# Gate panel 0 instead of gate panel 5 among the early products, in a fused hybrid-encoder step on one Trainium2 core

## The chip, the core and the metric

One core of one Trainium2 chip runs the whole program. The metric is the device time of one execution in microseconds (us). TensorE (PE) does matrix products, VectorE (DVE) and ScalarE (ACT) element-wise work, GpSimd (POOL) small work and some transfers, SyncE (SP) issues most DMAs. Each engine takes its instructions strictly in the order in which they were written for it.

## The reference

One layer, for 1024 prompt positions and 64 sample positions (together T = 1088), D = 1024 channels:

```
xn = rms_norm(x, g_pre);  z = xn @ w_in
xa, ga, q, k, v, gb, fl, ma, mb = split(z)
ua = causal_conv(xa)                          # width 4, per channel
r, i = sigmoid(block_diag(ua) + bias)         # two gates
a = exp(-8 r softplus(-a_param));  x_in = sqrt(1 - a^2) * i * ua
h_t = a_t h_(t-1) + x_in_t                    # the recurrence
ya = h * silu(ga)                             # branch a
yb = attention(q, k, v, logf) * silu(gb)      # branch b
mix = (sigmoid(ma) * (ya @ w_a) + sigmoid(mb) * (yb @ w_b)) @ w_o
h = x + rms_norm(mix);  h += rms_norm(sigmoid(h @ w_ple_gate) * (p @ w_ple_proj))
```

Branch a has 1024 channels, treated as eight panels of 128 channels, numbered 0 to 7. For panel k there is an x panel (columns of xa, the input of convolution and recurrence) and a gate panel (columns of ga, which multiply the recurrence's output through silu). Each is a product of the 1088 normalised positions with 1024 x 128 weights.

## The kernel before

All products are made in a split of float32 into a high and a low part, as three matmuls (high x high, low x high, high x low; lines L166 to L168). The stages that matter follow each other on TensorE.

**Products of halves.** Query and key columns go in pairs of panels through a Strassen-like scheme with seven products of half size (`seven`, L811, tiles `quad`). Four panels of branch a are made there too, two at a time: the x panel 0 with gate panel 1 in front of the queries and keys, and gate panels 3 and 5 behind them. Their results go to memory: x panel 0 to `d_x0`, gate panel k, with silu already applied, to `d_ga[k]`. Which gate panels are made early is in one table, `GA_EARLY`.

**Attention**, with dense panels of the merge gates as filler. It ends where the first panel of the next stage begins.

**The recurrence of branch a.** What is not made early is made here as *dense panels*: a panel is 72 matmuls, three chunks of columns (368, 368 and 352 wide) of 24 each, tile `acc`, and each chunk takes one of the 8 PSUM banks (`mm8`) until another engine has read it out. The list of dense panels is written out in the order x1, g0, x2, x3, g2, x4, x5, g4, x6, x7, g6, g7 (x for an x panel, g for a gate panel). For each of the eight k the steps are:

- the x panel's chunks are copied from PSUM to the tile `xp` (ScalarE, L84);
- convolution: one ScalarE step (`u<-xp`, L1662) and three on VectorE (L1666); for odd k the tiles carry an `_e`, for even k they don't;
- `u` is split into `uh` (ScalarE) and `ul` (VectorE);
- six small products for the two gates (tiles `gacc`, three matmuls each, one bank each), read out by six sigmoids on ScalarE (L1705, into `x` and `r`);
- decay and root: exponential (L1720), tanh (L1723), square root (L1740) on ScalarE; sigmoid, exponential/tanh and square root need different function tables, and a change of table is an `ACT_TABLE_LOAD`;
- state input and scan on VectorE (L1750, L1746, L1762), output y = h * silu(gate) (L1781), split into `yah` (ScalarE) and `yal` (VectorE);
- the gate panel: where it is dense, a sigmoid on ScalarE (L1811, `sg<-acc`) and a product on VectorE (L1814), which only then frees the bank; where it was made early, one DMA on SyncE's queue loads it from `d_ga` (L1821). The tile `sg` exists twice, for even and for odd k.

The order in which these steps are written for the engines is not fixed by hand: `go_all` is a list scheduler. It holds for each step an engine, a duration, what it depends on, the need for a free bank and the function table, and always takes the step that can begin first by these numbers, ties going to the step with the longest chain behind it. Dense panels stay in their order. Steps issued by TensorE take half a chunk (12 matmuls) or one gate product at a time.

**Held products.** The outputs `yah`, `yal` are multiplied with the first two panels of branch a's output projection (tiles `held`); the further panels, branch b's projection, the output projection and the final embedding stage follow on TensorE.

The lines that the change reaches:

```
GA_EARLY = (1, 3, 5)                                                     # L50
some = [(cols(C_XA, 1), ("r", d_x0))] + [(cols(C_GA + k * P, 1), ("g", d_ga[k])) for k in GA_EARLY]   # L227
mixed = [([s1, s2], (d1, d2)) for (s1, d1), (s2, d2) in (some[:2], some[2:])]
for k in range(KT):                                                      # the list of dense panels
    branch_a += [("x", k + 1)] if k + 1 < KT else []
    branch_a += [("g", k)] if k not in GA_EARLY else []
...
        if k in GA_EARLY:                                                # L1823, own_gate(k)
            step("S", 500.0, load, w=sgs(k), lag=4000.0)
        else:
            dense(("g", k), evac)
```

Of the kernel before, what the change touches and what calls it, by code (L numbers as in the profile page):

```python
# [46 lines left out]

AHEAD = 4000
WAKE = 30
GA_EARLY = (1, 3, 5)  # L50
LN1P = [1.0 / 15, 1.0 / 13, 1.0 / 11, 1.0 / 9, 1.0 / 7, 1.0 / 5, 1.0 / 3]


# [14 lines left out]
def hybrid_step(tc, a, o):  # L68
# [151 lines left out]
    def cols(c, n=2):  # L220
        return w_in[:, c:c + n * P]
# [4 lines left out]
    quads = [([cols(c + p * P)], ((t, p), (t, p + 1))) for p in range(0, NP, 2) for c, t in ((C_K, "k"), (C_Q, "q"))]  # L226
    some = [(cols(C_XA, 1), ("r", d_x0))] + [(cols(C_GA + k * P, 1), ("g", d_ga[k])) for k in GA_EARLY]  # L227
    mixed = [([s1, s2], (d1, d2)) for (s1, d1), (s2, d2) in (some[:2], some[2:])]
# [6 lines left out]
    for k in range(KT):  # L235
        branch_a += [("x", k + 1)] if k + 1 < KT else []
        branch_a += [("g", k)] if k not in GA_EARLY else []
    later = deque([(cols((C_XA if t == "x" else C_GA) + k * P, 1), ((t, k),)) for t, k in branch_a]
# [1224 lines left out]
    def step(engine, ns, do, r=(), w=(), lag=0.0, after=(), table=None, bank=0, ahead_of=0.0, frees=False):  # L1463
        i = len(todo)
        deps = set(after)
        for x in (*r, *w):
            deps |= {written[x]} if x in written else set()
        for x in w:
            deps |= read_by.get(x, set())
        for x in w:  # L1470
            written[x], read_by[x] = i, set()
        for x in r:
            if x not in w:
                read_by.setdefault(x, set()).add(i)
        todo.append((engine, ns, do, deps, lag, table, bank, ahead_of, frees))
        return i
# [61 lines left out]
    def sgs(k):  # L1538
        return [("sg", odd(k), c) for c in range(3)]
# [261 lines left out]
    def own_gate(k):  # L1801
# [20 lines left out]

        if k in GA_EARLY:  # L1823
            step("S", 500.0, load, w=sgs(k), lag=4000.0)
# [704 lines left out]
```

## Time and profile before

| what | us |
|---|---|
| three runs | 1425.78, 1425.80, 1425.51; median 1425.78 |
| the profiled execution: its span | 1425.7 |
| TensorE busy in it | 1401.0 (98%) |
| the recurrence and the held products, from the first dense panel to the last held product | 844.4 to 1034.0 |

The profiled execution's span, from its first to its last instruction, is within 0.1 us of the median of the runs, so nothing of weight lies around it. Times in rows are from the start of the span. Matmuls overlap: a row's duration is from its issue to its end, while the distance between the starts of neighbours tells the pace (368 columns: 0.17 us). An entry `[1.35 <-DVE y L1254]` at the end of a row is idle time of the engine before it and what ended it.

### The profile page before, as it was taken

The numbers are of one execution on the slowest core, as the hardware profiler recorded it, in microseconds if no ns is written. First come the engines' busy times: TensorE is split into PE (matmuls) and PEld (weight loads), VectorE is DVE, ScalarE is ACT, GpSimd is POOL, SyncE is SP. The second block draws the span as 40 slices with busy tenths as digits, with TensorE's granted clock in tenths as the row PEclk, the third lists the DMA queues.
The fourth block names the chain that finished last, engine by engine and source line by source line (L and its number), as shares of the span: only waits on it lengthen the run. The fifth ranks groups of instructions, "written<-read, shape, count | busy, mean of one in ns | idle before, by whom it ended". The sixth has DMA issues, their size and how long they took to land.

```text
span 1425.7 us, 24345 instructions
## 1 busy us (share of the span) xinstructions
PE 1401.0 (98%) x9063; PEld 1331.9 (93%) x9063; DVE 901.7 (63%) x1563; ACT 728.6 (51%) x1338; POOL 379.7 (27%) x485
## 2 busy tenths in 40 slices
PE   9999999999999999999999899999999999999996
PEld 8999999999999999999999889999999998888885
DVE  6546665665653466667676567798845866338644
ACT  5414444444332566666666558778624434324533
POOL 0002332423321355455544430010001564000000
PEclk9999999999999999999999999999999999999999
DMA  5376655655336858757567434242283667224111
GB/s 204 123 131 109 114 168 178 189 158 171 95 76 183 217 150 148 177 125 178 131 155 163 65 89 57 44 61 48 79 299 126 213 215 281 91 76 146 49 49 44
DMA packets 141074, 191.64 MB, mean 134 GB/s; under 512 B 24580, under 2 KB 99372, under 8 KB 140956
## 3 DMA queue, kind: packets, MB, share of 16 engines
q1 hardware_dynamic: 119308, 149.43, 42.7%
q10 hardware_dynamic: 17104, 27.32, 5.3%
q0 software_dynamic: 4544, 13.34, 3.3%
q8 instruction: 71, 1.16, 0.4%
q14 instruction: 47, 0.39, 0.1%
HBM read 127.11 MB, written 62.92 MB: 133 GB/s over the span
## 4 chain that ended last, share of the span: by engine, by line
PE 89%; DMA 5%; DVE 2%; ACT 1%; issue 1%; SPq 1%; POOL 0%; DVEq 0%; ACTq 0%; POOLq 0%
PE quad L811 19%; PE acc L166 13%; PE acc L167 12%; PE acc L168 12%; PE quad_b L2129 5%; PE tp L1196 4%; PE pv L1240 2%; PE pv L1238 2%; PE s L1171 2%; PE s L1170 2%; DMA d_ma<-st 1%; PE vacc L166 1%; DMA w_raw<-in_w_in 1%; PE vacc L167 1%; PE vacc L168 1%; DMA d_y<-y 1%
## 5 line engine op out<-in xcount | busy, mean ns | idle before, releaser
L166 PE MATMUL acc<-xh,wh 128*128 128x368 f32 (+1 forms) x672 | 228.0, 339 | 0.4
L167 PE MATMUL acc<-xl,wh 128*128 128x368 f32 (+1 forms) x672 | 220.1, 328 | 0.0
L168 PE MATMUL acc<-xh,wl 128*128 128x368 f32 (+1 forms) x672 | 219.7, 327 | 0.0
L166 PEld LDWEIGHTS acc<-xh,wh 128*128 128x128 f32 x672 | 126.8, 189 | 1.9 <-DVE nm L1150 1.3
L167 PEld LDWEIGHTS acc<-xl,wh 128*128 128x128 f32 x672 | 127.0, 189 | 0.6
L168 PEld LDWEIGHTS acc<-xh,wl 128*128 128x128 f32 x672 | 126.7, 189 | 0.0
L84 ACT ACTIVATE th<-tp 128x512 fp32r<-128x512 f32 (+1 forms) x160 | 86.6, 549 | 65.9 <-PE tp L1196 61.5
L87 DVE TENSOR_TENSOR tl<-tp,th 128x512 fp32r<-128x512 f32 (+1 forms) x160 | 99.2, 634 | 30.4 <-ACT th L84 29.1
L87 DVE TENSOR_TENSOR wl<-w_raw,wh 128x1024 fp32r<-128x1024 f32 (+1 forms) x67 | 76.8, 1148 | 59.6 <-ACT wh L84 40.8
L84 ACT ACTIVATE wh<-w_raw 128x1024 fp32r<-128x1024 f32 (+1 forms) x67 | 62.7, 938 | 91.2 <-PE quad L811 37.5
L811 PE MATMUL quad<-xh,wh 128*128 128x272 f32 x448 | 93.9, 291 | 0.0
L811 PE MATMUL quad<-xl,wh 128*128 128x272 f32 x448 | 92.6, 288 | 0.0
L811 PE MATMUL quad<-xh,wl 128*128 128x272 f32 x448 | 92.5, 288 | 0.0
L1156 POOL TENSOR_SCALAR pb<-pb,sm 128x640 f32<-128x640 f32 (+1 forms) x64 | 61.4, 960 | 95.1 <-DVE sm L1155 87.3
L1238 PE MATMUL pv<-tl,vv 128*128 128x512 f32 x192 | 70.8, 369 | 6.1 <-DVE y L1254 5.4
L1153 ACT ACTIVATE pb<-pb,nm 128x640 f32<-128x640 f32 (+1 forms) x64 | 63.3, 989 | 25.9 <-DVE nm L1150 23.2
L84 ACT ACTIVATE wh<-s 128x512 fp32r<-128x512 f32 x54 | 34.0, 631 | 74.6 <-PE quad L811 48.3
L811 PEld LDWEIGHTS quad<-xl,wh 128*128 128x128 f32 x448 | 70.6, 188 | 0.0
L811 PEld LDWEIGHTS quad<-xh,wh 128*128 128x128 f32 x448 | 70.2, 188 | 0.2
L811 PEld LDWEIGHTS quad<-xh,wl 128*128 128x128 f32 x448 | 70.4, 188 | 0.0
L1150 DVE CUSTOM_DVE_ANT_0 pb<-s,mask 128x640 f32<-128x640 f32 (+1 forms) x64 | 65.0, 1015 | 4.4 <-PE s L1171 4.2
L1170 PE MATMUL s<-k,q 128*128 128x128 f32 (+2 forms) x192 | 67.4, 358 | 0.0
(692 smaller groups left out, 3958.5 us busy)
## 6 DMA issues: line engine op xcount, KB each, us to landing
w_raw<-in_w_in SPq DMA_DIRECT2D x56, 256.0 KB
q<-d_q SPq DMA_DIRECT2D x48, 256.0 KB
k<-d_k SPq DMA_DIRECT2D x48, 256.0 KB
w_raw<-in_w_in SPq DMA_DIRECT2D x56, 128.0 KB
wraw<-in_w_in SPq DMA_DIRECT2D x24, 256.0 KB
w_raw<-in_w_branch SPq DMA_DIRECT2D x24, 256.0 KB
d_k<-oh ACTq DMA_DIRECT2D x16, 272.0 KB
d_k<-kl SPq DMA_DIRECT2D x16, 272.0 KB
```

Of the source, the lines that this page charges most:

```text
L84: return act.activation(out=out, in_=in_, func=AF.Copy, scale=scale)
L87: return eng.tensor_tensor(out=out, in0=in0, in1=in1, op=ALU.subtract)
L166: pe.matmul(out, ah, bh, start=start, stop=False)
L167: pe.matmul(out, ah, bl, start=False, stop=False)
L168: pe.matmul(out, al, bh, start=False, stop=stop)
L811: pe.matmul(acc[:, c, :CW], l[:, k, :], r[:, k, c * CW:(c + 1) * CW], start=(first and k == 0 and p == 0), stop=(k == 3 and p == 2), skip_ ...
L1150: at = book("D", now[0] + HOP_PE, per(D_MAX, n), lambda: dve.tensor_tensor_reduce(out=pr[:, :n], in0=s[:, :n], in1=m, scale=-1.0, scalar=- ...
L1153: at = book("A", at, per(A_EXP, n), lambda: act.activation(out=pr[:, :n], in_=pr[:, :n], func=AF.Exp, scale=-1.0, bias=nm, accum_out=sm))
L1156: return free, book("G", at, per(G_NORM, n), lambda: pool.tensor_scalar(out=pr[:, :n], in0=pr[:, :n], scalar1=sm, scalar2=1.0, op0=ALU.mul ...
L1170: pe.matmul(s[:, c0:c0 + w], t["q1"][:, q], t["k1"][:, c0:c0 + w], start=True, stop=False)
L1238: pe.matmul(pv[:, 512 - n:], v, tl[:, c:c + n], start=(j == 0), stop=False)
L2129: pe.matmul(acc[:, c, :CW], l[:, k, :], r[k // 2][:, k % 2, c * CW:(c + 1) * CW], start=(first and k == 0 and p == 0), stop=(k == 3 and p ...
```

## The change

The table of early gate panels names panel 0 in place of panel 5, in the same position:

```
-GA_EARLY = (1, 3, 5)
+GA_EARLY = (1, 3, 0)
```

So among the products of halves gate panel 0 is made together with gate panel 3, from other columns of the same weight matrix into `d_ga[0]`; and in the recurrence the list of dense panels reads x1, x2, x3, g2, x4, x5, g4, x6, g5, x7, g6, g7, while panel 0's gate is loaded and panel 5's no longer is. The numbers of matmuls, of DMAs and of steps stay the same. Up to the first dense panel every engine's instructions stand in the same order as before. Behind it the scheduler comes to another order on every engine. Three places of it follow; in them `u`, `r`, `x` without and with `_e` are the tiles for even and odd k.

SyncE's queue at the start of the recurrence (`sg` and `sg_e` are the tiles for the gate, `w_raw` a dense panel's weights, `g_raw` the small gate weights), as a piece of the difference:

```order
 L1821 DMA sg_e<-d_ga 128x1088
 L249 DMA w_raw<-in_w_in 128x2x128 x4
+L1821 DMA sg<-d_ga 128x1088
 L1613 DMA g_raw<-in_w_rg_a 64x64 x2
 L1613 DMA g_raw<-in_w_rg_x 64x64 x2
```

The load of gate panel 0 stands behind the first weights that this stage loads; the load of panel 5, further down, is gone.

ScalarE around the six sigmoids of k = 3 (`r_e<-gacc`, `x_e<-gacc`), before:

```order
L1720 ACT_TABLE_LOAD
L1720 ACTIVATE e<-r,nsp_93 128x1092
L84 ACTIVATE wh<-w_raw 128x1024
L1723 ACTIVATE r<-r,sp_92 128x1092
L1705 ACT_TABLE_LOAD
L1705 ACTIVATE r_e<-gacc,vt 128x368 x2
L1705 ACTIVATE x_e<-gacc,vt 128x368
L1705 ACTIVATE r_e<-gacc,vt 128x356
L84 ACTIVATE xp<-acc 128x368
L1705 ACTIVATE x_e<-gacc,vt 128x368
L1705 ACTIVATE x_e<-gacc,vt 128x356
L1811 ACTIVATE sg<-acc 128x368
```

The same place in the change, in two pieces that follow each other, the first from the copy of the second chunk of x4:

```order
L84 ACTIVATE xp<-acc 128x368
L1720 ACT_TABLE_LOAD
L1720 ACTIVATE e<-r,nsp_93 128x1092
L1723 ACTIVATE r<-r,sp_92 128x1092
L84 ACTIVATE wh<-w_raw 128x1024
```

```order
L84 ACTIVATE xp<-acc 128x288
L84 ACTIVATE xp<-acc 128x64
L1662 ACTIVATE u<-xp,vt 128x1092
L84 ACTIVATE fin<-xp 128x3 x2
L1705 ACT_TABLE_LOAD
L1705 ACTIVATE r_e<-gacc,vt 128x368 x2
L1705 ACTIVATE x_e<-gacc,vt 128x368
L1705 ACTIVATE r_e<-gacc,vt 128x356
L1705 ACTIVATE x_e<-gacc,vt 128x368
L1705 ACTIVATE x_e<-gacc,vt 128x356
L84 ACTIVATE uh<-u 128x1092
L1811 ACTIVATE sg<-acc 128x368
```

Two copies of x4 and the first step of the next convolution now stand between the tanh and the six sigmoids; the sigmoids of gate panel 2 (`sg<-acc`) stand behind the six in both.

TensorE at the same place in the change, from the fourth of the six gate products on (what a row waits for is in brackets; Activation is ScalarE):

```order
L166 MATMUL gacc<-uh,g_h 128x356 [waits Activation_49]
L167 MATMUL gacc<-ul,g_h 128x356
L168 MATMUL gacc<-uh,g_l 128x356
L166 MATMUL gacc<-uh,g_h 128x368 [waits PE_49,Activation_49]
L167 MATMUL gacc<-ul,g_h 128x368
L168 MATMUL gacc<-uh,g_l 128x368
L166 MATMUL gacc<-uh,g_h 128x356 [waits Activation_49]
L167 MATMUL gacc<-ul,g_h 128x356
L168 MATMUL gacc<-uh,g_l 128x356
```

The six products stand in one run directly behind the third chunk of x4; before, the first four stood behind a half chunk of x4, and 12 dense matmuls stood between the fourth and the fifth.

ScalarE at the six sigmoids of k = 5, before:

```order
L1740 ACT_TABLE_LOAD
L1740 ACTIVATE r<-r 128x1092
L84 ACTIVATE xp<-acc 128x368 x2
L1705 ACT_TABLE_LOAD
L1705 ACTIVATE r_e<-gacc,vt 128x368
L1705 ACTIVATE x_e<-gacc,vt 128x368
L1705 ACTIVATE r_e<-gacc,vt 128x368
L1705 ACTIVATE x_e<-gacc,vt 128x368
L1811 ACTIVATE sg<-acc 128x368
```

and in the change, where the first row copies the second chunk of x6:

```order
L84 ACTIVATE xp<-acc 128x368
L1740 ACT_TABLE_LOAD
L1740 ACTIVATE r<-r 128x1092
L1705 ACT_TABLE_LOAD
L1705 ACTIVATE r_e<-gacc,vt 128x368
L1705 ACTIVATE x_e<-gacc,vt 128x368
L1705 ACTIVATE r_e<-gacc,vt 128x368
L1705 ACTIVATE x_e<-gacc,vt 128x368
L1705 ACTIVATE r_e<-gacc,vt 128x356
L1705 ACTIVATE x_e<-gacc,vt 128x356
L1811 ACTIVATE sg<-acc 128x368 x2
```

The square root and its table now stand behind that copy, and all six sigmoids stand together. On TensorE the six products of k = 5 stand in one run behind the second chunk of x6 in the change. In all, ScalarE has 50 table loads where it had 47.

## The prediction

> **What bounds the kernel now.** The page first: who is busy, and for how long.
>
> ```profile
> span 1425.7 us, 24345 instructions
> PE 1401.0 (98%) x9063; PEld 1331.9 (93%) x9063; DVE 901.7 (63%) x1563; ACT 728.6 (51%) x1338; POOL 379.7 (27%) x485
> ```
>
> TensorE sets the time; what an edit gains or costs is what it takes from or adds to TensorE's waits. The change moves instructions only behind the first dense panel of the recurrence, so next the stretch table for that stage, and the waits of TensorE behind it (engine, line, what it waited for; us in total, times, longest):
>
> ```profile
> 844.40:1034.00 189.60, 189.60 (x1151) 189.60 (x1150) 155.96 (x162) 143.12 (x220) 15.93 (x39) 1.00 0.34 64
> PE acc L166 <- DVE s L2148: 1.0, 1, 1.0
> PE quad_b L2129 <- DVE s L2148: 0.3, 1, 0.3
> ```
>
> In the stage (columns: length, then busy us of PE, PEld, DVE, ACT, POOL, granted clock, DMA share, GB/s) TensorE is busy for all 189.60 us. There is no wait to remove, and the change takes no matmul away. From 1034 to the end TensorE waits 1.3 us. Two things follow. The change can gain at most about 1.3 us, and a wait that it puts into this stage goes to the end almost whole, because nothing behind it has slack to swallow it. The question is whether the new order makes TensorE wait.
>
> **The change part by part.**
>
> *What costs nothing.* The early product of panel 0 has the shape of panel 5's, in the same place: 0. The dense panel g5 has the 72 matmuls of g0: 0, as long as TensorE does not wait. VectorE and ScalarE do the same steps; the three more table loads at 1.28 us (rows below) are 3.8 us, and ScalarE idles for 189.6 - 143.1 = 46.5 us in the stage. That cover holds except where TensorE waits for a ScalarE step queued behind a table load; those places are priced below. On SyncE's queue the 544 KB load of `sg` now stands behind the first four weight loads; queued behind it are the small gate weights and the next panel's weights. Those came late for ScalarE before, too:
>
> ```profile
> 856.62 1.06 ACT L84 ACTIVATE wh<-w_raw 128x1024 fp32r<-128x1024 f32 x1 [2.21 <-DMA w_raw<-in_w_in]
> 857.71 1.22 DVE L87 TENSOR_TENSOR wl<-w_raw,wh 128x1024 fp32r<-128x1024 f32 x1 [2.69 <-ACT wh L84]
> ```
>
> They are split by 858.9, for the third panel, which TensorE begins two panels (2 x 11.8 us, 72 matmuls each) and 12 gate products (some 6 us) after 844.4, at 874. Some 15 us of slack, and the DMA share of the stage is 0.34: 0.
>
> *The first wait: gate products of k = 3.* There are 8 banks. In the change the six products stand directly behind the third chunk of x4. At that moment gate panel 2 holds three banks, since its own sigmoids stand behind the six on ScalarE; the first five products take the other five. The sixth can begin only when the first of the six sigmoids has read its bank out. When does TensorE arrive, and when is the sigmoid done? As TensorE never waits before this place, in either program, the same count of matmuls brings it to the same time, and I read the times off the rows of before. Up to the first product it has 414 matmuls behind it (five dense panels and three groups of 18): the 415th is the row at 912.61. The last matmul of the second chunk of x4 is the one at 908.58.
>
> ```profile
> 844.43 0.33 PE L166 MATMUL acc<-xh,wh 128*128 128x368 f32 x1
> ...
> 908.58 0.33 PE L168 MATMUL acc<-xh,wl 128*128 128x368 f32 x1
> ...
> 912.61 0.33 PE L166 MATMUL acc<-xh,wh 128*128 128x368 f32 x1
> ...
> 914.60 0.33 PE L166 MATMUL gacc<-uh,g_h 128*128 128x368 f32 x1
> ...
> 916.61 0.33 PE L166 MATMUL acc<-xh,wh 128*128 128x368 f32 x1
> ```
>
> From 914.60 to 916.61 four products take 2.01 us, so five take 2.51 and TensorE stands before the sixth at 912.61 + 2.51 = 915.12. On ScalarE everything between is queued behind the copy of x4's second chunk, which cannot start before that chunk ends, at 908.58 + 0.33 = 908.91. Then, from start to start in rows where the same steps follow each other:
>
> ```profile
> 865.51 1.28 ACT L1720 ACT_TABLE_LOAD   x1
> 866.81 1.21 ACT L1720 ACTIVATE e<-r,nsp 128x1092 f32<-128x1092 f32 x1
> 868.05 1.21 ACT L1723 ACTIVATE r<-r,sp 128x1092 f32<-128x1092 f32 x1
> 869.28 1.28 ACT L1705 ACT_TABLE_LOAD   x1
> ...
> 897.81 1.06 ACT L84 ACTIVATE wh<-w_raw 128x1024 fp32r<-128x1024 f32 x1 [2.97 <-PE acc L167]
> 898.77 0.51 ACT L84 ACTIVATE xp<-acc 128x288 f32<-128x288 f32 x2
> 899.37 1.31 ACT L1662 ACTIVATE u_e<-xp,vt 128x1092 f32<-128x1092 f32 x1
> 900.58 0.28 ACT L84 ACTIVATE fin<-xp 128x3 f32<-128x3 f32 x2
> 900.80 0.42 ACT L84 ACTIVATE g_h<-g_raw 128x256 fp32r<-128x256 f32 x1
> ...
> 924.18 0.46 ACT L84 ACTIVATE xp<-acc 128x368 f32<-128x368 f32 x1
> 924.53 1.20 ACT L1723 ACTIVATE r_e<-r_e,sp 128x1092 f32<-128x1092 f32 x1
> ...
> 942.42 1.28 ACT L1705 ACT_TABLE_LOAD   x1
> 943.71 0.57 ACT L1705 ACTIVATE r<-gacc,vt 128x368 f32<-128x368 f32 x1
> ```
>
> Copy 0.35 (924.18 to 924.53); table, exponential and tanh 3.77 (865.51 to 869.28); weight split, two copies, convolution step and two small copies 2.99 (897.81 to 900.80); table and first sigmoid 1.86 (942.42 to 943.71 + 0.57). Sum 8.97, so the bank is free at 917.88: **2.76 us** of wait. Before, the same sigmoids started 1.5 us after their first product (914.60), and the last two products came later by 12 matmuls:
>
> ```profile
> 914.83 1.28 ACT L1705 ACT_TABLE_LOAD   x1
> 916.12 1.02 ACT L1705 ACTIVATE r_e<-gacc,vt 128x368 f32<-128x368 f32 x2
> ```
>
> *The second wait: gate products of k = 5.* The same picture: gate panel 4 holds three banks, five products the others, and the sixth needs the first sigmoid. The six stand behind the second chunk of x6, 642 matmuls after the start: the row at 950.28, the one ahead of it at 950.12, both now 2.76 later.
>
> ```profile
> 950.12 0.33 PE L168 MATMUL acc<-xh,wl 128*128 128x368 f32 x1
> 950.28 0.32 PE L166 MATMUL acc<-xh,wh 128*128 128x352 f32 x1
> ...
> 983.92 1.28 ACT L1740 ACT_TABLE_LOAD   x1
> 985.22 1.12 ACT L1740 ACTIVATE r_e<-r_e 128x1092 f32<-128x1092 f32 x1
> 986.24 0.40 ACT L84 ACTIVATE g_h<-g_raw 128x256 fp32r<-128x256 f32 x1
> ```
>
> TensorE stands before the sixth at 950.28 + 2.76 + 2.51 = 955.55. ScalarE's chain begins with the copy of x6's second chunk, at 950.12 + 0.33 + 2.76 = 953.21: copy 0.35, table and root 2.32 (983.92 to 986.24), table and first sigmoid 1.86, sum 4.53, done at 957.74: **2.19 us**. Before, root and table lay ahead of the copies, and no product waited.
>
> *Starting again.* After an idle stretch the first two matmuls are further apart than usual: 0.34 us where 0.23 is the pace of 512 columns.
>
> ```profile
> 839.12 0.50 PE L1238 MATMUL pv<-tl,vv 128*128 128x512 f32 x1 [1.35 <-DVE y L1254]
> 839.46 0.40 PE L1240 MATMUL pv<-th,vv 128*128 128x512 f32 x1
> 839.69 0.60 PE L1196 MATMUL tp<-ident,pb 128*128 128x128 f32 x4
> ```
>
> That is 0.1 us for each wait, together 0.2.
>
> *What is late next.* The dense panels behind the waits, the held products and everything behind 1034 move by the sum. ScalarE and VectorE work on x2 to x5 one panel (11.8 us) earlier than before, which would help only where TensorE waits for them; in this stage it did so nowhere.
>
> *Sum.* 2.76 + 2.19 + 0.2 = 5.15 on the profiled execution's 1425.7 is 1430.9; its span is within 0.1 us of the median of the runs, 1425.78, so against that too **1430.9 us**, 0.36% more.
>
> *Bounds of what the trace does not show.* No wait for a bank by a gate product of this size stands in the trace of before. From below each of the two is 0, if a bank comes free otherwise; a gain is excluded, since TensorE has nothing left to save there. From above: a ScalarE step in the chain may itself be held by VectorE, and the longest such wait in the stage is
>
> ```profile
> ACT uh L84 <- DVE u L1666: 11.6, 3, 4.1
> ```
>
> 4.1 us, which at one of the places gives 1430.9 + 4.1 = 1435.0. I take the chains as summed: all their rows are plain back-to-back steps, and both start from an end of TensorE's own work.
>
> **The rivals.**
>
> *The banks come free in time, no wait: 1425.8, not slower.* The place is the sixth product of k = 3. It decides itself by ScalarE's chain: TensorE needs 915.12 - 908.91 = 6.2 us from the end of x4's second chunk to the sixth product, and the wait is gone when the chain takes no more than that instead of 8.97. For it: before, TensorE passed all eight gates without a wait. Against it: engines work in order, the chain's first step is a copy of a chunk that TensorE has only just made, and leaving out even the whole convolution step (1.31) and the weight split (1.06) leaves 6.6. At k = 5 the same would need 4.53 to come down to 2.3. One wait without the other gives 1428.0 (only the second) or 1428.6 (only the first).
>
> *The wait costs TensorE its clock.* In the trace of before one idle stretch is followed by half the granted clock (the column ahead of the DMA share), a shorter one (1.35 us, above) is not:
>
> ```profile
> 809.00 0.79 PE L1238 MATMUL pv<-tl,vv 128*128 128x512 f32 x1 [4.05 <-DVE y L1254]
> 808.00:812.00 4.00, 3.00 (x11) 2.70 (x12) 3.72 (x14) 3.03 (x10) 0.77 (x2) 0.50 0.00 0
> 812.00:816.00 4.00, 4.00 (x19) 3.92 (x18) 1.75 (x4) 2.31 (x5) 1.28 (x2) 0.69 0.01 2
> ```
>
> 4.05 us of idleness cost half of 3.0 busy us and 0.31 of 4.0: 2.7 us. The first wait, 2.76, lies between 1.35 and 4.05; if it were enough, the time would be 1430.9 + 2.7 = 1433.6. Being nearer the lower of the two, and the second wait shorter still, I give it little. [...]
>
> *The chain is longer (VectorE holds ScalarE):* 1435.0, as bounded above.
>
> *Faster.* The earlier x panels would have to take away waits of TensorE; behind 844 there are 1.3 us, so 1424.5 at best, which is no change that can be told.
>
> **How the numbers follow.** About 0.2% (2.9 us) is what a measurement of this kernel can tell from no change. Forecast, both waits: 0.72. No wait: 0.08; one wait: 0.08 (about on the border, two thirds of it within 0.2%). Clock: 0.04. Longer chain: 0.05. Faster in some way that I don't see: 0.03. Slower is then 0.72 + 0.04 + 0.05 + 0.03 = 0.84, less a little for waits of which each comes out half a microsecond or more shorter: 0.82. Within 0.2%: 0.15, faster 0.03. The likeliest case's own range is 1429.3 to 1432.5 (each wait give or take some 0.7, the two sums of durations being good to about that). The range for 8 in 10 reaches down to the single waits and up to the clock case: 1428.0 to 1434.0.
>
> **What would show it.** TensorE's waits in the stage: two at L166 on `gacc`, each ended by ScalarE's sigmoid L1705, 2.8 us near 918 and 2.2 us near 958; the first held product at 1015.6 instead of 1010.5; nothing new behind it; granted clock 1.00 in the stage. Wrong if no `gacc` wait stands there, if a wait has another releaser (weights `wl`, a DMA, `ul`), or if the held products begin 5 us late and the end does not.

## The result, and the profile after

The changed kernel took 1428.88 us (median of 21 runs, 1424.38 to 1431.93) beside 1425.58 us (1423.59 to 1427.41, 21 runs) of the kernel before: a ratio of 1.0022, 95% interval 1.0016 to 1.0029. That is 3.3 us slower, inside the predicted range and 2.0 us below the predicted time. The two waits that were forecast came, but the sum around them was wrong in two places that nearly cancel, so the closeness of the number is in part luck. One execution of experiment 5 took 1719.66 us at a granted clock of 0.751 and is left out of the comparisons.

First the page of the changed kernel's profiled execution (1428.84 us, span 1427.1), then TensorE's waits in the recurrence, and those behind it:

```profile
span 1427.1 us, 24346 instructions
PE 1401.5 (98%) x9063; PEld 1333.2 (93%) x9063; DVE 903.1 (63%) x1563; ACT 733.6 (51%) x1341; POOL 378.2 (26%) x485
...
PE gacc L166 <- ACT r_e L1705: 5.1, 2, 2.7
...
PE acc L166 <- DVE s L2148: 1.0, 1, 1.0
PE quad_b L166 <- DVE s L2000: 0.7, 1, 0.7
```

The recurrence has two new waits, and both are where the prediction put them: at the sixth gate product of k = 3 and of k = 5, ended by the first of ScalarE's sigmoids. Their rows in the timeline, with the last matmul ahead of each:

```profile
907.28 0.33 PE L168 MATMUL gacc<-uh,g_l 128*128 128x368 f32 x1
910.31 0.43 PE L166 MATMUL gacc<-uh,g_h 128*128 128x356 f32 x1 [2.70 <-ACT r_e L1705]
...
949.55 0.32 PE L168 MATMUL gacc<-uh,g_l 128*128 128x356 f32 x1
952.24 0.66 PE L166 MATMUL gacc<-uh,g_h 128*128 128x356 f32 x1 [2.37 <-ACT r_e L1705]
```

Now the recurrence whole, from its first matmul to the first held product, before and after (columns as in the stretch table above):

```profile
844.43:1010.51 166.08, 166.08 (x1010) 166.08 (x1009) 135.38 (x140) 131.25 (x203) 12.15 (x32) 1.00 0.33 56
836.67:1011.50 174.83, 169.76 (x1010) 169.06 (x1009) 142.22 (x147) 137.59 (x209) 12.36 (x34) 0.98 0.33 58
```

It became 8.75 us longer, not 5.15. It also began 7.76 us earlier, and what stands behind it takes 415.63 instead of 415.20 us. So -7.76 + 8.75 + 0.43 makes the +1.4 us by which the two profiled executions differ. (The runs differ by 3.3 because the first profile of before is of a dear execution: a run's time is some 1.7 us above its span in every run that has both on record, here 1428.84 for 1427.1. A span of 1425.7 therefore belongs to a run of about 1427.4, and not to one of the median, as the text ahead of the prediction has it.) Two things have to be explained: 3.6 us more in the recurrence, and an earlier start that the prediction did not have at all.

**The 3.6 us more is the clock.** Stretches about the two waits (granted clock ahead of the DMA share):

```profile
908.00:911.00 3.00, 0.69 (x4) 0.70 (x5) 2.92 (x4) 2.97 (x7) 0.00 (x0) 1.00 0.64 82
911.00:914.50 3.50, 3.50 (x14) 3.50 (x13) 3.46 (x4) 3.27 (x8) 1.11 (x3) 0.51 0.05 12
914.50:918.00 3.50, 3.50 (x22) 3.50 (x21) 2.37 (x5) 1.60 (x5) 0.31 (x1) 1.00 0.04 9
...
952.00:955.50 3.50, 3.26 (x11) 3.26 (x12) 3.43 (x3) 3.50 (x10) 0.00 (x0) 0.51 0.00 0
955.50:959.00 3.50, 3.50 (x24) 3.50 (x23) 1.76 (x3) 1.37 (x5) 0.00 (x0) 1.00 0.00 0
```

Behind each wait 3.41 us run at half the clock (0.50 in 911.09 to 914.50 and in 952.05 to 955.46), which loses about 1.7 us each time. Waits 5.07, clock 3.4 and 0.3 for starting again make the 8.75.

**The earlier start comes from the end of the attention.** Three stretches of before, then the same of the changed kernel:

```profile
794.00:798.00 4.00, 4.00 (x26) 3.42 (x25) 2.82 (x5) 2.35 (x5) 3.68 (x6) 1.00 1.03 44
798.00:802.00 4.00, 4.00 (x30) 3.86 (x29) 2.54 (x7) 3.08 (x7) 3.83 (x7) 1.00 0.99 45
802.00:806.00 4.00, 2.95 (x22) 2.57 (x20) 0.69 (x1) 0.02 (x1) 0.17 (x1) 1.00 0.93 130
```

```profile
794.00:798.00 4.00, 4.00 (x25) 3.29 (x24) 3.28 (x6) 2.18 (x5) 3.70 (x7) 1.00 0.97 151
798.00:802.00 4.00, 4.00 (x31) 3.97 (x30) 2.37 (x6) 2.44 (x6) 3.15 (x5) 1.00 0.58 122
802.00:806.00 4.00, 4.00 (x30) 3.81 (x29) 3.26 (x11) 3.35 (x9) 0.34 (x1) 1.00 0.00 1
```

The last two columns differ. Before, the DMA engines are busy until 806 (a share of 0.93 and more) and move only 44 to 45 GB/s until 802; after, they move 122 to 151 GB/s and are done by 802. SyncE's queue in 790 to 808 (packets, MB, share of the 16 engines), before and after, says that it is the same amount of data in both:

```profile
q1 hardware_dynamic: 1616, 0.79, 67.3%
...
q1 hardware_dynamic: 1616, 0.79, 30.2%
```

And this is ScalarE's copy that starts the sum for y, in both; it may overwrite `y` only when the transfer of the last `y` has left:

```profile
807.63 0.59 ACT L84 ACTIVATE y<-pv 64x512 f32<-64x512 f32 x1 [5.61 <-DMA d_y<-y]
...
802.09 0.59 ACT L84 ACTIVATE y<-pv 64x512 f32<-64x512 f32 x1 [0.93 <-DMA d_y<-y]
```

The load in front of that transfer is the weights of the second dense panel, issued at 791.7. Before, that panel is g0; now g0 is an early product, and the second dense panel is x2. The same number of bytes takes less than half the time, the transfer of `y` lands in 5.9 instead of 10.6 us, and TensorE's wait of 4.05 us at 809 with its 2.7 us of clock is gone. That place makes 6.9 of the 7.76 us: the same matmul is 0.86 us earlier than before ahead of it, from small waits near the start, and 7.73 us earlier behind it. (The waits of 1.35 us at 831 in the changed kernel and 839 in before, on the same line, are of the next `y`.)

The slow load itself has not vanished. The changed kernel needs gate panel 0's columns earlier, among the products of halves, and loads them there at the place where before loads gate panel 5's. The same stretch in before and in the changed kernel:

```profile
310.00:314.00 4.00, 4.00 (x34) 4.00 (x33) 2.98 (x4) 3.08 (x5) 0.00 (x0) 1.00 0.30 112
...
310.00:314.00 4.00, 4.00 (x34) 4.00 (x34) 3.77 (x5) 2.27 (x4) 0.00 (x0) 1.00 0.99 43
```

The DMA engines are full there (a share of 0.99) at 43 GB/s, but TensorE is busy for all 4.00 us in both. So the change moved a slow load from a place where TensorE waits for what stands behind it to one where it does not.

### The profile page after: what moved, and what is told of

The parts are those of the page before. It is cut to its first block, busy times and chain, and to the rows that moved or that the text cites. A ratio compares the mean times of both kernels' runs of the same rounds, so it can differ in the third digit from the quotient of the medians.

```text
span 1427.1 us, 24346 instructions
## 1 busy us (share of the span) xinstructions
PE 1401.5 (98%) x9063; PEld 1333.2 (93%) x9063; DVE 903.1 (63%) x1563; ACT 733.6 (51%) x1341; POOL 378.2 (26%) x485
## 4 chain that ended last, share of the span: by engine, by line
PE 90%; DMA 4%; DVE 2%; ACT 2%; issue 1%; SPq 1%; POOL 0%; DVEq 0%; ACTq 0%; POOLq 0%
PE quad L811 19%; PE acc L166 13%; PE acc L167 12%; PE acc L168 12%; PE quad_b L2129 5%; PE tp L1196 4%; PE pv L1240 2%; PE pv L1238 2%; PE s L1171 2%; PE s L1170 2%; PE vacc L458 1%; DMA d_ma<-st 1%; DMA w_raw<-in_w_in 1%; PE vacc L166 1%; PE vacc L167 1%; PE vacc L168 1%
```

## The experiments

**1. The two kernels once more.** Is the dear place in the attention a chance of one execution?

> The kernel before, unchanged, to learn how much its single executions differ. In its first profile TensorE waited 4.05 us at 809 (product of values, for VectorE's y, which waited for the transfer of y) and lost 2.7 us of clock behind it; in the changed kernel's profile the same place cost 1.35 us, at a full clock, though the program is the same there. Theory A (that place varies from execution to execution, and the first profile of before was a dear one): this profile shows a wait below 3 us there, and the recurrence, from its first matmul to the first held product, takes 166.1 us again, +-0.4. Theory B (the place costs before 6 to 7 us always, and the change made it cheaper): 4 us and half the clock again. Time 1425.6 by both.

> The changed kernel once more. Theory A: recurrence from its first matmul to the first held product 174.8 us +-1 (166.1, two waits of 2.7 and 2.4, two stretches of 3.4 us at half the clock), the place at 809 between 1.3 and 4.1 us, time 1428.9. Theory B: the place at 809 shows 1.3 us again at full clock. A third reading, that the half clock in the first profile was chance and not a consequence of the waits: recurrence 171.4 us, full clock behind at least one of the two waits.

Before again: 1425.23 us, ratio 0.9998 (0.9989 to 1.0007). The changed kernel again: 1428.30 us, ratio 1.0017 (1.0008 to 1.0026). TensorE's waits and one stretch of before again, then the recurrence of the changed kernel again:

```profile
PE pv L1238 <- DVE y L1254: 4.7, 2, 3.4
...
798.00:802.00 4.00, 4.00 (x30) 3.85 (x29) 2.55 (x7) 3.08 (x7) 3.83 (x7) 1.00 1.02 45
```

```profile
837.38:1012.43 175.05, 169.99 (x1011) 169.28 (x1009) 142.23 (x147) 137.59 (x209) 13.47 (x34) 0.98 0.34 58
```

Theory A, that the first profile of before had bad luck there, falls: 45 GB/s and a wait of 3.4 us again, and no wait at all at that place in the changed kernel's second profile. Theory B holds: the place costs before 5.3 us in this profile and 6.9 in the first, and the change took that away. The half clock behind both waits came again too.

**2. Whose columns are loaded.** In before, one address is changed, and the reverse in the changed kernel (only the part of the line that changes is printed):

```diff
 # kernel before, list of the dense panels' weights
-    (cols((C_XA if t == "x" else C_GA) + k * P, 1), ((t, k),))
+    (cols(C_GA + 6 * P if (t, k) == ("g", 0) else (C_XA if t == "x" else C_GA) + k * P, 1), ((t, k),))
 # changed kernel
+    (cols(C_GA if (t, k) == ("x", 2) else (C_XA if t == "x" else C_GA) + k * P, 1), ((t, k),))
```

> The kernel before with one number of an address changed: its dense panel g0 reads the weight columns of gate 6 instead of those of gate 0 (so gate 0's output is made from the wrong weights; every instruction, size and queue is the same). Theory A (the load of gate 0's columns, which before issues at 791.7 in the attention, is slow: DMA engines 1.0 busy at 44 GB/s until 806, and holds up the transfer of y behind it): the load is done near 802, TensorE's wait at 806 to 809 falls from 3.4 to 4.1 us to about 1.3, the clock stays 1.00 there, time 1420 to 1421.5. Rival (where the load stands in the queues makes the wait, not which columns it reads): wait 3.4 us or more again, 1425.6.

> The reverse: the changed kernel, whose panel x2 (the one that it loads in the attention, at 790.8) reads the columns of gate 0 instead (so branch a's x panel 2 is wrong; all instructions as in the changed kernel). Theory A: DMA engines full at 44 GB/s to about 805, TensorE waits 3.4 to 4.1 us near 808 and loses some clock behind it, time 1428.6 + 4 to 7 = 1432.5 to 1435.5. Rival: wait 1.3 us, 1428.6.

Before with gate 6's columns: 1419.90 us against 1426.47 of before, ratio 0.9956 (0.9943 to 0.9968). The changed kernel with gate 0's columns in x2's place: 1433.74 us, ratio 1.0062 (1.0049 to 1.0076), some 5 us above the changed kernel in the series before. SyncE's queue in 790 to 808 in the first and in the second, and the second's waits for y:

```profile
q1 hardware_dynamic: 1616, 0.79, 27.9%
```

```profile
q1 hardware_dynamic: 1616, 0.79, 67.8%
...
PE pv L1238 <- DVE y L1254: 5.3, 2, 3.9
```

With every instruction in its place, the address alone takes 6.6 us from the one kernel and adds 5 us to the other. In the first, no wait is left at that place (the theory had 1.3 us, which is the next `y`'s), and its recurrence begins at 836.86, as early as the changed kernel's. So the earlier start is caused by which panel's columns are loaded in the attention, and by nothing that the change moved in the queues.

The second kernel shows something more. Its two waits in the recurrence are as long as the changed kernel's, but no half clock follows. Their rows, a stretch behind the first, and the whole recurrence:

```profile
917.21 0.43 PE L166 MATMUL gacc<-uh,g_h 128*128 128x356 f32 x1 [2.70 <-ACT r_e L1705]
...
957.87 0.43 PE L166 MATMUL gacc<-uh,g_h 128*128 128x356 f32 x1 [2.59 <-ACT r_e L1705]
...
917.00:921.00 4.00, 3.79 (x23) 3.79 (x24) 3.96 (x4) 3.79 (x8) 1.11 (x3) 1.00 0.12 21
...
843.42:1015.67 172.25, 166.96 (x1010) 166.06 (x1009) 141.94 (x147) 137.65 (x209) 12.37 (x34) 1.00 0.34 59
```

172.25 us, 6.2 more than before instead of 8.75. So the clock does not hang on the length of a wait alone, which is what the next experiment asks. It also means that this profile understates the address: its recurrence begins 6.8 us later than in the changed kernel's first profile, and then is 2.6 us shorter for want of the half clock.

**3. How long may TensorE idle?** Behind the kernel before, bursts of matmuls that each wait for a VectorE step (without the special case of the first burst; the shorter sweep has bursts of 50 and 55 and steps of 1600 to 2000 elements):

```diff
+    for burst in (48, 53, 58):
+        for w in range(300, 3072, 300):
+            sub(dve, zw[:, :w], zero[:, :w], zero[:, :w])
+            acc = mm.tile([P, 512], F32, name="sweep", tag="acc")
+            for i in range(burst):
+                pe.matmul(acc[:, :], zi[:, :], zw[:, :512], start=i == 0, stop=i == burst - 1)
```

> The kernel before, and behind it 30 bursts of 48, 53 or 58 matmuls of 512 columns (11 to 13 us at full clock), each burst made to wait for a VectorE step of 300 to 3000 elements, so for idle stretches of some 0.6 to 3.6 us. Theory (an idle stretch of some length always halves the clock): full clock behind all stretches to some 1.5 to 2.3 us, a half-clock stretch of 3.4 us behind all longer ones, the same for the three burst lengths. Rival (it depends on how the stretch lies to a window that runs freely): stretches of the same length halve the clock in some of the three and not in others, over a band of lengths. [...]

> The kernel before with a shorter tail: ten bursts of 50 or 55 matmuls behind VectorE steps of 1600 to 2000 elements, idle stretches of 1.6 to 2.0 us. Theory (the clock is set for windows of 3.41 us that run on a fixed grid, and falls to half behind a window in which TensorE idled for about 1.8 us or more): with the grid read from the clock's own changes, every stretch with 1.81 us or more in one window is followed by half clock, none with 1.76 or less. Rival (length of the stretch alone): all stretches above one length and none below. And a second question: in the longer sweep, whose part ahead of the bursts is the kernel before, the load of gate 0's columns in the attention was fast and TensorE waited only 1.3 us there. If that load's speed hangs on where the program's length puts the tensors in memory, it can be fast or slow here; if the longer sweep was a chance, it is slow: 3.4 to 4.1 us near 806.

Two bursts of the longer sweep and the stretch behind each:

```profile
1497.01 11.14 PE L2496 MATMUL sweep<-zw,zi 128*128 128x512 f32 x48 [2.53 <-DVE zw L87]
1613.26 13.95 PE L2496 MATMUL sweep<-zw,zi 128*128 128x512 f32 x53 [1.81 <-DVE zw L87]
...
1497.10:1504.00 6.90, 6.90 (x31) 5.71 (x32) 0.00 (x0) 0.00 (x0) 0.00 (x0) 1.00 0.00 0
1613.30:1620.00 6.70, 6.70 (x22) 5.34 (x23) 0.00 (x0) 0.00 (x0) 0.00 (x0) 0.75 0.00 0
```

An idle stretch of 2.53 us left the clock alone, one of 1.81 us halved it. In the trace's record of the granted clock all changes in one execution lie a whole number of 3.413 us apart (the changed kernel's at 911.09, 914.50, 952.05 and 955.46: 1, 11 and 1 of them). I cut each idle stretch at the grid on which they lie, into windows of 3.413 us, and took the largest piece that lies in one window:

```
                              largest piece in one window   stretches   followed by half clock
longer sweep                  0.56 to 1.76 us               15          0
longer sweep                  1.81 to 3.29 us               14          14
shorter sweep                 1.27, 1.36, 1.66, 1.82, 1.91  5           0
shorter sweep                 1.90, 1.91, 2.23, 2.33        4           4
changed kernel, both profiles 2.63, 2.18, 2.04, 2.37        4           4
changed, gate 0's columns     1.72, 1.41                    2           0
```

(Left out is the long idle time ahead of each sweep's first burst.) The smallest piece with half clock behind it has 1.81 us, the largest without has 1.91. The waits of 2.70 and 2.37 us in the changed kernel held a piece of 2.04 us or more in both profiles; with gate 0's columns those of 2.70 and 2.59 us were cut by an edge of the grid to 1.72 and 1.41, and the clock stayed at 1.00. The theory of the longer sweep falls, since length alone decides nothing between 1.81 us (halved above) and 2.75 us (1.00 in the 7 us behind it); the rival, by which it depends on how the stretch lies to a window, holds. The border that the shorter sweep's theory gave was too sharp: two pieces of more than 1.81 us, 1.82 and 1.91, left the clock alone. The wait of 4.05 us in the kernel before lies in two windows, 2.73 us in the one and 1.33 in the next, and its half clock lasts from 807.67 to 814.50, 6.83 us.

The second question of the shorter sweep had an unforeseen answer. In the part that is the kernel before, gate 0's load was neither as slow nor as fast as it had been. SyncE's queue took 51.9% of 790 to 808 for the same packets, `y` landed in 7.1 us, and TensorE waited 0.7 us; in the longer sweep it waited there not at all. That part's instructions are the same in all three programs. So the columns alone do not settle the load's speed; the runs do not show what else does. The three series ran on three different chips, but before took 1426.02, 1426.47 and 1426.11 us on them, which a fast load would have put 5 to 7 us lower, so the chip alone is not it. Of each sweep there is one execution only, so chance is not excluded for them.

**4. Make the gate panels later.** If a finished gate panel's three banks are what the sixth product lacks, it should be enough to make that panel later. A table gives the order of the x panels' work (c2: convolution step of panel 2, x4: dense panel x4), and the dense panels become x1 x2 x3 x4 g2 x5 x6 g4 x7 g5 g6 g7:

```diff
+PATHS = ("c0 x1", "c1 x2", "c2 x3 c3 x4", "", "c4 x5 c5 x6", "", "c6 x7", "c7")
...
-        branch_a += [("x", k + 1)] if k + 1 < KT else []
+        branch_a += [("x", int(s[1])) for s in PATHS[k].split() if s[0] == "x"]
...
-        convolve(k)
-        if k + 1 < KT:
-            x_path(k + 1)
+        for s in PATHS[k].split():
+            (convolve if s[0] == "c" else x_path)(int(s[1]))
```

> The change kept, but the dense gate panels g2 and g4 stand one x panel later (x1 x2 x3 x4 g2 x5 x6 g4 x7 g5 g6 g7), so that at the products of k = 3 and k = 5 no finished gate panel holds three banks. My theory (banks held by a finished gate panel make the sixth product wait, the wait halves the clock): no wait at the gate products, clock 1.00, recurrence 166.1 us, time 1425.6, within 0.1% of before. Rival (ScalarE is late because of the three more table loads, whatever holds the banks): a wait of 2 us or more for a sigmoid remains at k = 3 or 5, time above 1427.5.

1421.19 us (6 runs), ratio 0.9968 (0.9957 to 0.9980) to before: it beats both kernels, and my expectation by 4 us. Its recurrence, and the table loads of one of ScalarE's lines, which are five here and four in the changed kernel:

```profile
837.42:1003.99 166.57, 166.49 (x1011) 166.18 (x1009) 140.84 (x146) 137.38 (x210) 12.73 (x34) 1.00 0.34 61
...
L1811 ACT ACT_TABLE_LOAD x5 | 6.4, 1283 | 0.1
```

TensorE is busy for 166.49 of 166.57 us at full clock, and no wait of a `gacc` stands in the list. ScalarE has one table load more than in the changed kernel, so the number of table loads alone does not make the waits.

But the edit did not take the holder of the banks away. The last chunk of g2 is now made some 2 us ahead of the first product of k = 3 instead of 12, and its banks still come free only behind all six products. The first product and the read-out of g2:

```profile
907.75 0.33 PE L166 MATMUL gacc<-uh,g_h 128*128 128x368 f32 x1
...
916.41 1.42 DVE L1814 TENSOR_TENSOR sg<-acc,sg 128x368 f32<-128x368 f32 x3
```

At k = 5 it is the same with g4: products from 949.26 on, banks free from 965.04 on. What changed is the order about them. At k = 3 and k = 5 half a chunk stands between the fourth and the fifth product, as it did before, and ScalarE's sigmoids come sooner behind the first product. So this run shows what the two waits cost, and not that the three banks are needed for them.

That is shown by rows within the changed kernel. At k = 4 its sigmoids come far later than at k = 3, and TensorE does not wait. There the last bank of g2 is read out just ahead of the first product, which the rows show in this order, with the first sigmoid behind them:

```profile
917.65 0.53 DVE L1814 TENSOR_TENSOR sg<-acc,sg 128x352 f32<-128x352 f32 x1 [1.10 <-ACT sg L1811]
918.53 0.33 PE L166 MATMUL gacc<-uh,g_h 128*128 128x368 f32 x1
...
931.91 0.57 ACT L1705 ACTIVATE r<-gacc,vt 128x368 f32<-128x368 f32 x1
```

The same reading for other places (us from the start of the first product to the start of the first sigmoid):

```
                         finished gate panel    first sigmoid   six products in one run   wait
changed kernel, k = 2    none                   5.72            yes                       0
changed kernel, k = 3    g2 holds three banks   4.83            yes                       2.70
changed kernel, k = 4    none                   13.38           yes                       0
changed kernel, k = 5    g4 holds three banks   4.41            yes                       2.37
before, k = 3            g2 holds three banks   1.52            no                        0
panels later, k = 3      g2 holds three banks   0.71            no                        0
panels later, k = 5      g4 holds three banks   2.85            no                        0
```

A late sigmoid without a finished gate panel makes no wait (k = 2 and k = 4), and a finished gate panel with sooner sigmoids and half a chunk among the products makes none either. In the two places that wait, the late sigmoid and the finished panel come together, with nothing among the products that TensorE could do meanwhile. Which of the three a cheaper edit should remove was not tried one by one.

What I had not counted in the time is that x2's load stays in the attention here, so the change's gain there is kept: it is 4.8 us below the before of its series. Against the changed kernel in the same series, 1428.30 - 1421.19 = 7.1 us is the mean price of the two waits with their clock, together with whatever else the order changed.

**5. One place alone.** Only g2 is made later (`"c4 x5", "c5 x6"` in the table above).

> The change with g2 alone one x panel later (x1 x2 x3 x4 g2 x5 g4 x6 ...): the first of the two places is relieved, g4 still holds its banks at k = 5. My theory: no wait at k = 3; at k = 5 one wait, and a longer one, since g4 is finished earlier against ScalarE: 4.7 us near 961, with half the clock behind it; recurrence 166.1 + 4.7 + 1.7 to 3.4 = 172.5 to 174.2 us. Rival (each place has its price for itself): 2.4 us at k = 5, recurrence 170.2. Time 1427.5 to 1430 by both.

> The changed kernel with g2 alone one x panel later, once more, since its first profile was of a disturbed execution. Theory (banks; one wait is left, at k = 5, for which g4's three banks are held; g4 is finished earlier against ScalarE than in the changed kernel): one wait of 4.2 to 4.7 us near 955 to 961, and 3.4 or 6.8 us at half clock about it, since it idles TensorE for more than 1.8 us of at least one window of 3.41 us wherever the windows lie; recurrence 166.5 + 4.4 + 1.0 to 2.7 = 172 to 173.7 us. Rival (each place has its price for itself): 2.4 us, recurrence 169 to 170.5.

1426.96 us, ratio 1.0011 (1.0002 to 1.0020). The profile of the second run (one execution, 1429.23 us), the wait in its recurrence and the stretches about it:

```profile
PE gacc L166 <- ACT r_e L1705: 4.8, 1, 4.8
...
954.00:958.00 4.00, 1.50 (x5) 1.50 (x6) 4.00 (x4) 3.97 (x7) 0.55 (x3) 0.58 0.00 0
958.00:962.00 4.00, 4.00 (x16) 4.00 (x15) 3.97 (x4) 3.14 (x7) 0.56 (x1) 0.57 0.00 0
```

One wait at k = 5, of 4.8 us instead of 2.37, and some 6.8 us at half clock (0.58 and 0.57 over these 8 us); the recurrence took 173.5 us, as expected. Relieving one place saved little, and the rival, that each place has its price for itself, falls. The reason is not only that TensorE comes to k = 5 sooner. Counted from the start of the recurrence, it stands before the sixth product after 112.5 us instead of 113.2, but the first sigmoid ends after 117.3 instead of 115.5: the six products now stand behind the third chunk of x6, and on ScalarE that chunk's copies and the next convolution step stand ahead of the square root. These 0.7 and 1.7 us are the 2.4 that the wait grew by.

**6. The attention's gain without the change.** The kernel before, with its own early panels 1, 3 and 5, loads x2 ahead of g0 (`"c0 x1 c1 x2", "", "c2 x3 c3 x4", ""` in the table).

> The kernel before with its own early gate panels 1, 3, 5, but the dense panels in the order x1 x2 g0 x3 x4 g2 x5 g4 x6 x7 g6 g7, so that x2 and not g0 is loaded in the attention. Theory A: wait near 806 about 1.3 us at full clock, as in the changed kernel: 1420.5 to 1421.5, and on top one wait of 1.7 us for a bank near 885 (g0 holds three) with or without half clock behind it: 1422 to 1425. Rival (the early product of panel 0 is what helped the attention): wait 3.4 us or more near 806, 1427 to 1429.

1426.42 us, ratio 1.0004 (0.9995 to 1.0013): a miss by at least 1.4 us. TensorE's waits in the profile:

```profile
PE acc L166 <- ACT r L1705: 2.0, 1, 2.0
...
PE pv L1238 <- DVE y L1254: 1.3, 1, 1.3
...
PE gacc L166 <- ACT g_h L84: 1.2, 1, 1.2
...
PE gacc L167 <- DVE ul L87: 0.7, 2, 0.5
```

The attention went as theory A has it: no wait but the 1.3 us of the next `y`, and the rival falls. But g0's load, now at 842.6, is slow there too: SyncE's queue is at 80.0% of 842 to 862 where before it was at 51.3% of its own 848 to 866. ScalarE waits for these weights, and what stands behind their split comes late with it:

```profile
856.96 1.06 ACT L84 ACTIVATE wh<-w_raw 128x1024 fp32r<-128x1024 f32 x1 [7.79 <-DMA w_raw<-in_w_in]
```

Counted from the start of the recurrence that row is 17.9 us in, where before it was 12.2. The split `g_h` of the small gate weights, further down ScalarE's order, starts 6 us later by the same count, and TensorE waits 1.2 us for it. There is besides the wait of 2.0 us for a bank that I had expected (1.7); the execution's mean granted clock is 0.996, where that of experiment 4, without such a wait, is 0.997. The recurrence took 173.6 us. That the 1.2 us would vanish with a fast load was not tried.

## Why the prediction was right, and where it was not

*What bounds the kernel.* Right: the recurrence had no slack, and all that was put into it passed on. The end behind 1034 swallowed nothing.

*The two waits.* Right, as mechanism and as size: 2.70 us for 2.76 and 2.37 for 2.19, at the products and with the releaser that were named. The cause is read from the rows: five products pass, the sixth waits for the first sigmoid, and the products of k = 2 and k = 4, whose sigmoids come later still but beside no finished gate panel, do not wait. Experiment 4 removed the waits by another order, with the holder of the banks still there; its expectation has that wrong. Their times, near 910 and 952, are some 6 to 8 us earlier than foretold, and the first held product came at 1011.5 instead of 1015.6; that was the sign that something ahead of the recurrence had moved.

*Starting again.* 0.1 us each was the right size for the matmuls, but the price of starting again was the clock. The step that failed is the rival "the wait costs TensorE its clock", to which I gave 0.04 because 2.76 us was said to lie nearer 1.35 (no loss) than 4.05 (loss). That reading was wrong in itself: it is 1.41 us from the one and 1.29 from the other. In experiment 3 the border lies at 1.81 to 1.91 us within a window of 3.41 us, and four of the six waits of 2.37 to 2.70 us in its table were followed by half clock, at 1.7 us each. An estimate from that border: a wait of 2.70 us escapes when the edge cuts it between 0.9 and 1.8 us, 0.9 / 3.41 = 26% of the cases, one of 2.37 in 36%; 1.7 x (0.74 + 0.64) = 2.3 us on average. The term "sum 5.15" should have been 5.1 + 0.3 + 2.3 = 7.7; experiment 4 measured 7.1. The runs bear the variation out: one such window lowers the mean granted clock of an execution by some 0.0012, and the changed kernel's runs average 1431.3 us at 0.994 (4 runs), 1429.5 at 0.995 (9), 1428.2 at 0.996 (11) and 1426.3 at 0.997 (7); one run at 0.998, with 1428.9 us, does not fit.

*What costs nothing.* Here the larger mistake stands, and the forecast did not see its sign. "The change moves instructions only behind the first dense panel" is true of the order on the engines, and the rows of SyncE's queue read alike in both kernels. But the row at 791.7 means g0's columns before and x2's now, and while these load, the DMA engines move 44 against 122 to 151 GB/s. The row of 4.05 us at 809 was in the prediction, taken for the clock only; what made TensorE wait there was not followed back to the transfer of `y` and the load ahead of it. Experiment 2 measured that term, which the sum put at nothing, at 6.6 us in the one direction and 5 in the other.

*Faster.* "In some way that I don't see" existed, with 5 to 7 us; it only was not larger than the waits with their clock. 7.1 lost, 6.6 won and 0.4 to 0.9 more behind the recurrence give about +1; the two comparisons gave +3.3 and +2.3. A remainder of 1 to 2 us is not settled: the attention's price (6.9 and 5.3 us in two profiles) and the clock's (a mean of 0.994 to 0.998) both vary from one execution to the next, and the runs' own spread (7.6 us of the changed kernel, 3.8 of before) is larger than it.

## What to carry to other kernels

When an edit changes which block is worked on when, follow the loads by their addresses, not by their names: here two rows that read alike loaded different columns while the DMA engines moved 44 or 122 to 151 GB/s, and the transfer of `y` behind the slow load landed in 10.6 us instead of 5.9. Follow every wait of the bounding engine that already stands in the profile back to its first cause, even far from the edit, since a change can take it away as well as add one. In this kernel a new wait of TensorE of 2.4 us or more is to be priced with 1.7 us of clock on top (four of six lost it), and the smallest piece in one window with half clock behind it had 1.81 us. A panel finished long before its reader is ready is not early work but a holder of banks; it cost 2.70 and 2.37 us where the next products' reader was late too and TensorE had no other matmul in between. And when an edit is to take a cause away, look in its trace whether the cause is gone, and not only whether the wait is.

## What the runs showed of the hardware that I had not expected

- Cut at the grid of 3.413 us on which its changes lie, TensorE's granted clock was half behind every window at full clock with 2.04 us or more of idleness and behind none with 1.76 or less (29 stretches of the longer sweep, 9 of the shorter, the six waits of the changed kernel and of its variant with gate 0's columns); in between it varied: 1.81 us was followed by half clock, 1.82 was not. In the changed kernel, with 0.19 us of idleness in the half-clock window itself, the half clock lasted 3.41 us; in before, with 1.33 us, 6.83.
- Loads of 512 KB from one weight matrix, with the same shape and in the same place of the queue, kept SyncE's queue busy for 67.3% or 27.9% of 18 us in the one kernel and 30.2% or 67.8% in the other, by the columns read alone. For one and the same panel the share also changed with a tail added to the program: 67.3%, 51.9% and, in the longer sweep, 31.4% (there with some packets more). Why is open.
